# First loads on two queues, last outputs shared with GpSimd, last activations in another ring, one activation and one down product placed later

## The chip, the cores and the metric

The kernel runs on one core of one Trainium2 chip. The metric is the device time of one execution in microseconds (us). A core has TensorE (PE, matmuls; PEld is its weight load), VectorE (DVE), ScalarE (ACT), GpSimd (POOL) and SyncE (SP, which here only issues transfers). Each engine works through its own list of instructions in order and waits on semaphores for the others.

## The reference

A decoder trunk of two layers (`DEPTH`) on x of 512 tokens and 1024 features. Each layer mixes tokens with two kinds of attention, and then comes an MLP with a squared ReLU, the part that matters here; the last step is an RMSNorm.

```python
def hybrid_layer(x, norm_mix, w_in, ...):
    h = rmsnorm(x, norm_mix)
    proj = h @ w_in
    ...
    mixed = jax.nn.sigmoid(gate_a) * y_a + jax.nn.sigmoid(gate_b) * y_b
    x = x + mixed @ w_out
    h = rmsnorm(x, norm_mlp)
    return x + jnp.square(jax.nn.relu(h @ w_up)) @ w_down      # 1024 -> 4096 -> 1024

def reference(x, ..., norm_final):
    for l in range(DEPTH):
        x = hybrid_layer(x, ...)
    return rmsnorm(x, norm_final)
```

## The kernel before

Data lie transposed, features on the 128 partitions and the 512 tokens along the free axis, so x is eight tiles of 128x512. Every fp32 operand is split into a high part and the rest (`h`, `lo`), and a product is three matmuls per block of 128: high by high, high by low and low by high (L212 to L214 in `gemm`). ACT makes the high part by a cast (`wh` L186 for weights, `uh` L234 for x times gain, `sh` L1215 for the operands of the fast product, `oh` L1296 for activations); DVE makes the rest (`wl` L187, `ul` L235, `sl` L1216), but for the activations GpSimd does (`ol` L1297). PSUM has eight banks of 512 columns, which go by the tags mm, S, PT and O, two each, and are taken in turn by `bank()`.

Weights come by `fetch` (L170: a DMA of a plan's next piece into a buffer `raw`), then `convert` splits them into `wh` and `wl` one step ahead of their use.

**The MLP.** The first 8 of the 32 up products of a layer are made plainly. The other 24 are made in 12 units, g = 4 to 15, each of which gives two blocks of 128 features, called z and y, by seven half-size products (class `Strassen`, `unit`). One such product is eight matmuls (L1226). Products 0, 2 and 4 of a unit go to one bank `m`, one after the other, with ACT copying the bank out in between (L1250 for product 0, L1258 for product 2); products 1 and 6 share another (L1254). L1261 copies product 3. DVE puts the pieces together, `halves` (L1286) folds them, and `act` does Relu (L1294), Square (L1295) and the cast to `oh` (L1296) on ACT and the rest `ol` (L1297) on GpSimd. Meanwhile `convert` of the class makes the seven operands of the next unit, two of the sums on GpSimd (L1206, L1207).

The down products (`down`, twelve matmuls each: four blocks of activations by three; x takes them at L949) come in 48 pieces, six groups of eight; group c reads activations 4c to 4c+3. Twelve run ahead of the units. The others are placed between the products of the units: at each of four spots (ahead of products 2, 4 and 6 and at the end) `between` may run one, and a tuple says how many each unit gets. What is left runs after unit 15. The last eight activations (units 12 to 15) are read by a last set of products (`wdn`) after that.

The rings of buffers that matter: `oh` and `ol`, eight each (activations); `uh` and `ul`, eight each (x times gain, and the seven operands of a unit); `t2`, `raw`.

**The start.** `go` issues the transfer of the gains, then x and the halves of the first weight (`wva`) alternate on SP; 20 matmul instructions on a tile of ones (L1106) run while they come. `token_proj` (L315) makes the first products, x being the stationary side; per x tile it needs `uh`, `ul`, `wh` and `wl`.

**The tail.** The last layer's products are made in two halves of 256 tokens. `out(f)` works out the row factors R of half f by matmuls into a PSUM bank (`rstd`, L283), multiplies the eight tiles of x by R (L1067) and sends them out in five transfers (L1068).

An automatic scheduler in the toolchain puts the final order of each engine together from the program's order, so an instruction can stand elsewhere than the text has it.

Of the kernel before, what the change touches and what calls it, by code (L numbers as in the profile page):

```python
# [12 lines left out]
F32R = mybir.dt.float32r  # L13
AF = mybir.ActivationFunctionType
OP = mybir.AluOpType
AX = mybir.AxisListType

L = 2
D = 1024
T = 512  # L20
KT = D // 128
# [122 lines left out]
class Body:  # L144
# [19 lines left out]
    def fetch(self):  # L164

        if self.plan:
            src, n, *tag = self.plan.popleft()
            tag = tag[0] if tag else self.raws.popleft() if self.raws else "raw"
            raw = self.t(tag, [128, 1024], name="raw")
            self.nc.sync.dma_start(raw[:, :n], src)  # L170
            self.loaded.append((raw, src, n))

    def convert(self):
# [28 lines left out]

    spots = ()
    raws = deque()

    def gemm(self, ps, w, k0, xs, ks=8, start=True, stop=True):
        h, lo = w
# [85 lines left out]
    def token_proj(self, srcs, n, banks, u):  # L293
        mm = self.nc.tensor.matmul
        for c in range(4):
            first = len(srcs[c]) == 2
            parts = []
            for j in range(2):
                if len(u) <= 2 * c + j:
                    self.first_u(u, 2 * c + j)  # L300
                if first:
                    h, lo = self.weights(srcs[c][j], n)
                    parts.append((h[:, :n], lo[:, :n]))
            if not first:
                h, lo = self.weights(srcs[c][0], 2 * n)
                if len(srcs[0]) == 2 and c == 1:
                    self.setup()
                parts = [(h[:, j * n:(j + 1) * n], lo[:, j * n:(j + 1) * n]) for j in range(2)]
            for j in range(2):
                uh, ul = u[2 * c + j]  # L310
                h, lo = parts[j]
                first, last = c == 0 and j == 0, c == 3 and j == 1
                for b in range(NB):
                    s = slice(b * 128, (b + 1) * 128)
                    mm(banks[b][:, :n], uh[:, s], h, start=first, stop=False)  # L315
                    mm(banks[b][:, :n], uh[:, s], lo, start=False, stop=False)
                    mm(banks[b][:, :n], ul[:, s], h, start=False, stop=last)
                if j == 0:
                    self.ahead()
                yield  # L320
# [607 lines left out]
    def mlp(self, l, x, u, acc, gm):  # L928

        nc, a = self.nc, self.a  # L930
        R = None
        pend = []
        acts = []

        def act(ps):
            t = self.t("tmp", [128, T])
            nc.vector.scalar_tensor_tensor(t, ps, 0.0, R, op0=OP.max, op1=OP.mult)
            h = self.t("oh", [128, T], F32R)
            lo = self.t("ol", [128, T], F32R)
            nc.scalar.activation(t, t, AF.Square)  # L940
            nc.scalar.copy(h, t)
            nc.vector.tensor_tensor(lo, t, h.bitcast(F32), op=OP.subtract)
            acts.append((h, lo))

        def down(c, m, w):

            ps = self.bank()
            yield from self.gemm(ps, w, 4 * (m % 2), acts[4 * c:4 * c + 4], ks=4)
            nc.vector.tensor_add(x[m], x[m], ps)  # L949

        def downs():
            for c in range(6):
                for m in range(8):
                    if m % 2 == 0:
                        w = self.weights(a["wd2"][l, c, m // 2])
                    yield lambda: run(down(c, m, w))

        S = Strassen(self, l, x, gm)
        D = downs()
        raws = [None] * 16  # L960
        g0 = self.PLAIN // 2
        S.load(g0)
        for j in range(self.PLAIN):
# [12 lines left out]
            for _ in range(3):  # L976
                next(prep, None)
        conv = S.convert(g0)
        for i in range(12):
            next(D)()  # L980
            if i < 7:
                next(prep, None)
                next(prep, None)
            elif i == 7:
                run(prep)
            else:
                next(conv, None)
                next(conv, None)
            if i == 10:
                S.load(g0 + 1)  # L990
        run(conv)
        for g, n in zip(range(g0, 16), (2, 2, 3, 3, 4, 4, 4, 4, 4, 3, 1, 0)):
            S.load(g + 2)
            S.unit(g, D, n, acts)
        for d in D:
            d()
        u_next = []
        acts = acts[24:]
        if l + 1 < L:
            acc = []  # L1000
            self.load_small(l + 1)
            for m in range(8):
                ps = self.bank()
                w = self.weights(a["wdn"][l, m].rearrange("p k c -> p (k c)"))
                run(self.gemm(ps, w, 0, acts))
                nc.vector.tensor_add(x[m], x[m], ps)
                acc = self.sumsq(x[m], acc, m == 7)
                u_next.append(self.make_u(x[m], self.gain[:, 16 * l + 16:16 * l + 24], m))
                nc.scalar.dma_start(self.xs[m], x[m])
        else:  # L1010
            self.last(x, acts, a["wdn"][l])
        self.acc = acc
        return u_next

    def last(self, x, acts, wdn):


        nc, a = self.nc, self.a
        n = T // 2
# [39 lines left out]
            nc.scalar.activation(xm, xm, AF.Copy, scale=self.gain[:, 32 + m:33 + m])  # L1059

        def out(f, wait):
            R, _ = self.rstd(acc[f], (self.turn_tag(), self.turn_tag()), wait=wait, exp=False, copy=f == 0)
            for k, w in ((0, 1), (1, 1), (2, 2), (4, 2), (6, 2)):
                y = self.t("t2", [128, 2, n], name="y")[:, :w]
                for j in range(w):
                    eng = nc.gpsimd if f == 0 and k + j in (0, 3, 5, 7) else nc.vector
                    eng.tensor_tensor(y[:, j], x[k + j][:, f * n:(f + 1) * n], R, op=OP.mult)  # L1067
                nc.sync.dma_start(a["yT"][f, :, k:k + w], y)  # L1068

        acc = [[], []]  # L1070
        run(chain(*[products(0, m) for m in (0, 2, 3, 4, 5, 6, 7)]))
# [18 lines left out]
    def first_u(self, u, k):  # L1090
        x = self.t("t2", [128, T], name="x")
        self.nc.sync.dma_start(x, self.a["xT"][k])
        u.append(self.make_u(x, self.gain[:, :8], k))
        self.acc = self.sumsq(x, self.acc, k == KT - 1)

    def go(self):
        nc, a = self.nc, self.a
        self.gain = self.cp.tile([128, 40], F32, name="gain")
        nc.sync.dma_start(self.gain, a["gain"])
        self.ones2 = self.cp.tile([128, 2], F32, name="ones")  # L1100
        nc.vector.memset(self.ones2, 1.0)
        ones = self.t("tmp", [128, 128], name="ones")
# [9 lines left out]
        self.plan = deque(x for l in range(L) for x in self.order(l))  # L1112
        self.loaded, self.split = deque(), deque()
        self.raws = deque(("e", "e"))
        for l in range(L):
            u = self.layer(l, u)
            self.x_src = self.xs


class Strassen:  # L1120
# [9 lines left out]
    def __init__(self, body, l, x, gm):  # L1130
        self.b, self.nc, self.l, self.x, self.gm = body, body.nc, l, x, gm
        self.raw, self.ops = {}, {}

    def prepare(self, R):

# [94 lines left out]
    def unit(self, g, D, n, acts):  # L1230
        b, nc = self.b, self.nc
# [16 lines left out]
        m = product(0)  # L1248
        y = b.t("zz", [128, 2, 512], name="y")
        A.copy(y[:, 0], m)  # L1250
        next(conv, None)
        p5 = product(1)
        z = b.t("zz", [128, 2, 512], name="z")
# [9 lines left out]
        between()  # L1263
        product(4, m)
        V.tensor_tensor(z, z, m[:, None, :].to_broadcast([128, 2, 512]), op=OP.add)
        pair = [None, None]
        self.act(self.halves(z), pair, 0)
        next(conv, None)
        p2 = product(5)
        V.tensor_tensor(y[:, 0], p2, y[:, 0], op=OP.subtract)  # L1270
# [1 line left out]
        between()  # L1272
        product(6, p5)
        V.tensor_tensor(y[:, 1], y[:, 1], p5, op=OP.subtract)
        self.act(self.halves(y), pair, 1)
        acts += pair
        next(conv, None)
        between()
        for _ in conv:
# [6 lines left out]
        self.nc.vector.tensor_tensor(c.rearrange("p (k c) -> p k c", k=2), v[:, :, 0], v[:, :, 1], op=OP.add)  # L1286
        return c

    def act(self, c, pair, i):

        b, nc = self.b, self.nc
        h = b.t("oh", [128, T], F32R)
        lo = b.t("ol", [128, T], F32R)
        nc.scalar.activation(c, c, AF.Relu)  # L1294
        nc.scalar.activation(c, c, AF.Square)  # L1295
        nc.scalar.copy(h, c)  # L1296
        nc.gpsimd.tensor_tensor(lo, c, h.bitcast(F32), op=OP.subtract)  # L1297
        pair[i] = (h, lo)


def chain(*gens):
# [33 lines left out]
```

## Time and profile before

| | |
|---|---|
| time, median of 3 runs | 1535.23 us (1534.68 to 1535.87) |
| the profiled execution | 1534.54 us; span in the trace 1532.5 us |
| granted TensorE clock | 0.998 |
| PE busy | 1515.8 us, 99% of the span |
| DVE, ACT, POOL busy | 74%, 53%, 14% |

A timeline row gives start, length, engine, line, operation, output tile <- input tiles, shape, and in brackets the idle time ahead of it and what ended it. A row of waits gives who waited for what, the total in us, how often, and the longest. SPq is the queue of SP's instructions. PE matmuls are pipelined: the time from one start to the next counts, not the length.

```profile
span 1532.5 us, 21386 instructions
```

### The profile page before, as it was taken

To read this page: it belongs to the slowest core of one execution; us is meant where nothing else is said; L and a number is where in the kernel's file an instruction comes from. 1 tells how busy PE (TensorE), PEld (TensorE's weight loads), DVE (VectorE), ACT (ScalarE), POOL (GpSimd) and SP (SyncE) were. 2 spreads that over 40 slices of the span, in tenths; PEclk is the share of its full clock that TensorE was granted. 3 is DMA by queue.
4 is the path that set the end of the run, shared out by engine and by line. 5 is a ranking of instruction groups with operands and counts; after the bars stand their busy time and mean duration, and the time that the engine had idled before them with its cause. 6 is when DMAs were issued, how large, how long until landed. Compare 5 with 4: busy or idle time off the path is not lost.

```text
span 1532.5 us, 21386 instructions
## 1 busy us (share of the span) xinstructions
PE 1515.8 (99%) x7772; PEld 1270.9 (83%) x7772; DVE 1132.8 (74%) x2191; ACT 816.8 (53%) x1529; POOL 216.8 (14%) x178
## 2 busy tenths in 40 slices
PE   9999999999999999999999999999999999999997
PEld 8878888888888888888888788878888888888887
DVE  5588998866479887775646799887574989877753
ACT  6464665553454655555435556565434646555652
POOL 4000000000201332221300000000002023222222
PEclk9999999999999999999999999999999999999999
DMA  7655422143333333322546543222422333323221
GB/s 263 176 149 136 120 70 83 64 136 101 99 95 112 110 97 101 106 69 79 176 141 175 156 128 86 85 67 70 151 97 97 95 113 109 105 92 107 69 83 56
DMA packets 56633, 169.49 MB, mean 111 GB/s; under 512 B 7344, under 2 KB 8112, under 8 KB 56528
## 3 DMA queue, kind: packets, MB, share of 16 engines
q1 hardware_dynamic: 53072, 161.84, 34.5%
q10 hardware_dynamic: 3456, 6.29, 1.2%
q8 instruction: 61, 1.00, 0.3%
q14 instruction: 44, 0.36, 0.1%
HBM read 140.77 MB, written 4.19 MB: 95 GB/s over the span
## 4 chain that ended last, share of the span: by engine, by line
PE 90%; DVE 4%; ACT 3%; issue 1%; DMA 1%; POOL 1%; SPq 0%; DVEq 0%; ACTq 0%; POOLq 0%
PE ps_mm L212 12%; PE ps_mm L213 12%; PE ps_mm L214 12%; PE ps_S L1226 4%; PE ps_O L1226 4%; PE ps_O L447 4%; PE ps_PT L212 3%; PE ps_PT L214 3%; PE ps_PT L213 3%; PE ps_PT L421 3%; PE ps_PT L1226 3%; PE ps_mm L1226 3%; PE ps_S L213 2%; PE ps_S L214 2%; PE ps_S L212 2%; PE ps_O L213 2%
## 5 line engine op out<-in xcount | busy, mean ns | idle before, releaser
L186 ACT CAST wh<-raw 128x1024 fp32r<-128x1024 f32 (+2 forms) x187 | 192.4, 1029 | 251.7 <-PE ps_mm L213 66.0
L187 DVE TENSOR_TENSOR wl<-raw,wh 128x1024 fp32r<-128x1024 f32 (+2 forms) x187 | 225.3, 1205 | 55.1 <-ACT wh L186 54.0
L212 PE MATMUL ps_mm<-uh,wh 128*128 128x512 f32 x512 | 202.2, 395 | 0.0
L213 PE MATMUL ps_mm<-ul,wh 128*128 128x512 f32 x512 | 201.5, 394 | 0.0
L214 PE MATMUL ps_mm<-uh,wl 128*128 128x512 f32 x512 | 201.3, 393 | 0.0
L399 ACT ACTIVATE E<-E,mx 128x128 f32<-128x128 f32 x192 | 107.8, 562 | 65.8 <-DVE mx L398 62.7
L213 PE MATMUL ps_mm<-ol,wh 128*128 128x512 f32 (+1 forms) x316 | 122.9, 389 | 0.8 <-POOL ol L1297 0.8
L212 PE MATMUL ps_mm<-oh,wh 128*128 128x512 f32 (+1 forms) x316 | 122.9, 389 | 0.1
L214 PE MATMUL ps_mm<-oh,wl 128*128 128x512 f32 (+1 forms) x316 | 122.3, 387 | 0.0
L1216 DVE TENSOR_TENSOR sl<-s,sh 128x512 fp32r<-128x512 f32 x96 | 93.8, 980 | 34.3 <-ACT sh L1215 33.8
L430 ACT CAST pth<-ps_PT 128x512 fp32r<-128x512 f32 x144 | 72.9, 512 | 81.9 <-PE ps_PT L421 81.4
L214 PEld LDWEIGHTS ps_mm<-uh,wl 128*128 128x128 f32 x512 | 96.3, 188 | 19.9
L212 PEld LDWEIGHTS ps_mm<-uh,wh 128*128 128x128 f32 x512 | 96.2, 188 | 18.4 <-issue 1.5
L213 PEld LDWEIGHTS ps_mm<-ul,wh 128*128 128x128 f32 x512 | 96.6, 189 | 14.9
L398 DVE CUSTOM_DVE_ANT_0 E<-ps_S,ct 128x128 f32<-128x128 f32 x192 | 91.5, 481 | 21.6 <-PE ps_S L395 20.3
L431 DVE TENSOR_TENSOR ptl<-ps_PT,pth 128x512 fp32r<-128x512 f32 x144 | 85.5, 596 | 28.3 <-ACT pth L430 27.6
L253 POOL TENSOR_TENSOR acc<-sq 128x512 f32<-128x512 f32 (+1 forms) x6 | 8.1, 1356 | 578.6 <-DVE wl L187 565.7
L421 PE MATMUL ps_PT<-ct,E 128*128 128x128 f32 x480 | 83.5, 274 | 0.0
L1215 ACT CAST sh<-raw 128x512 fp32r<-128x512 f32 x72 | 44.7, 621 | 64.3 <-PE ps_PT L1226 24.7
L1215 ACT CAST sh<-s 128x512 fp32r<-128x512 f32 x96 | 59.5, 620 | 29.0 <-PE ps_S L1226 9.1
L1216 DVE TENSOR_TENSOR sl<-raw,sh 128x512 fp32r<-128x512 f32 x72 | 61.5, 854 | 14.7 <-ACT sh L1215 14.2
L421 PEld LDWEIGHTS ps_PT<-ct,E 128*128 128x128 f32 x480 | 60.1, 141 | 13.6 <-issue 3.7
(421 smaller groups left out, 3966.3 us busy)
## 6 DMA issues: line engine op xcount, KB each, us to landing
raw<-wb SPq DMA_DIRECT2D x64, 512.0 KB, 3.6
raw<-wup SPq DMA_DIRECT2D x64, 512.0 KB, 3.5
raw<-wd SPq DMA_DIRECT2D x48, 512.0 KB, 3.6
kd<-hl SPq DMA_DIRECT2D x48, 256.0 KB, 5.4
w<-w SPq DMA_DIRECT2D x32, 256.0 KB, 4.5
q<-hl SPq DMA_DIRECT2D x64, 128.0 KB, 2.6
raw<-wo SPq DMA_DIRECT2D x16, 512.0 KB, 3.6
raw<-wout SPq DMA_DIRECT2D x16, 512.0 KB, 3.5
```

Source lines behind the costliest of these rows:

```text
L186: nc.scalar.copy(h[:, :n], raw[:, :n])
L187: nc.vector.tensor_tensor(lo[:, :n], raw[:, :n], h[:, :n].bitcast(F32), op=OP.subtract)
L212: mm(ps, h[:, c], xh, start=start and i == 0, stop=False)
L213: mm(ps, h[:, c], xl, start=False, stop=False)
L214: mm(ps, lo[:, c], xh, start=False, stop=stop and i == ks - 1)
L398: nc.vector.tensor_tensor_reduce(e, ps[:, :n], self.mask[:, T - n:], -1.0, BIG, OP.add, OP.min, mx)
L399: nc.scalar.activation(e, e, AF.Exp, bias=mx, scale=-1.0, accum_out=sm[:, i:i + 1])
L421: nc.tensor.transpose(ps[:, j * 128:(j + 1) * 128], E[i][:, b * 128:(b + 1) * 128], self.ident)
L431: nc.vector.tensor_sub(lo[:, o:o + n], ps[:, :n], h[:, o:o + n].bitcast(F32))
L1215: nc.scalar.copy(h, src)
L1216: nc.vector.tensor_tensor(lo, src, h.bitcast(F32), op=OP.subtract)
L1226: mm = lambda o, w, x, **kw: self.nc.tensor.matmul(o, w, x, skip_group_check=True, **kw)
```

## The change

1. **Start.** The transfer of x tile 0 goes out first and the gains follow it. The first piece of weights (half 0 of `wva`) is issued by ACT instead of SP, ahead of ACT's table load. For the first chunk the square of x (`sumsq`) is placed behind the weight's conversion. In the scheduled order ACT then casts half 0 ahead of making `uh` of tile 0, and PE runs its products strictly bank by bank (high-high, high-low, low-high; before, four high-high products came first).
2. **Units.** The activation of y (Relu, Square, cast, `ol`) is kept and issued in the next unit behind the copy of product 0 (L1250); in unit 15 at once.
3. **Placement.** Unit 5 gets one down product instead of two, so each later down stands one place further back, and three instead of two run after unit 15.
4. **Ring.** In the last layer the activations of units 14 and 15 go into the `uh`/`ul` ring instead of the `oh`/`ol` ring.
5. **Tail.** R stays in PSUM for DVE; ACT makes a copy in SBUF for GpSimd in both halves. GpSimd makes tiles 6 and 7, sent from ACT's queue, DVE makes 0 to 5, sent from SP. (Before, in the first half GpSimd made 0, 3, 5 and 7 and R was copied to SBUF for all; in the second DVE made all eight from PSUM; SP sent everything.)

```diff
@@ fetch
-            self.nc.sync.dma_start(raw[:, :n], src)
+            eng = self.nc.scalar if self.first else self.nc.sync
+            self.first = False
+            eng.dma_start(raw[:, :n], src)
@@ token_proj
+                x = None
                 if len(u) <= 2 * c + j:
-                    self.first_u(u, 2 * c + j)
+                    x = self.first_u(u, 2 * c + j)
+                if x is not None and not first:
+                    self.acc = self.sumsq(x, self.acc, 2 * c + j == KT - 1)
                 if first:
                     h, lo = self.weights(srcs[c][j], n)
                     parts.append((h[:, :n], lo[:, :n]))
+                    self.acc = self.sumsq(x, self.acc)
@@ the units
-        for g, n in zip(range(g0, 16), (2, 2, 3, 3, 4, 4, 4, 4, 4, 3, 1, 0)):
+        for g, n in zip(range(g0, 16), (2, 1, 3, 3, 4, 4, 4, 4, 4, 3, 1, 0)):
@@ out
-            R, _ = self.rstd(acc[f], ..., wait=wait, exp=False, copy=f == 0)
-            for k, w in ((0, 1), (1, 1), (2, 2), (4, 2), (6, 2)):
+            R, _ = self.rstd(acc[f], ..., wait=wait, exp=False, copy=False)
+            r = self.t("r", [128, T], name="R")[:, :n]
+            nc.scalar.copy(r, R)
+            for k, w in ((6, 2), (0, 1), (1, 1), (2, 2), (4, 2)):
                 y = self.t("t2", [128, 2, n], name="y")[:, :w]
                 for j in range(w):
-                    eng = nc.gpsimd if f == 0 and k + j in (0, 3, 5, 7) else nc.vector
-                    eng.tensor_tensor(y[:, j], x[k + j][:, f * n:(f + 1) * n], R, op=OP.mult)
-                nc.sync.dma_start(a["yT"][f, :, k:k + w], y)
+                    eng, R_ = (nc.gpsimd, r) if k == 6 else (nc.vector, R)
+                    eng.tensor_tensor(y[:, j], x[k + j][:, f * n:(f + 1) * n], R_, op=OP.mult)
+                (nc.scalar if k == 6 else nc.sync).dma_start(a["yT"][f, :, k:k + w], y)
@@ first_u, go
         self.nc.sync.dma_start(x, self.a["xT"][k])
+        if k == 0:
+            self.nc.sync.dma_start(self.gain, self.a["gain"])
         u.append(self.make_u(x, self.gain[:, :8], k))
-        self.acc = self.sumsq(x, self.acc, k == KT - 1)
+        return x
...
-        nc.sync.dma_start(self.gain, a["gain"])
...
+        self.fetch()
         for l in range(L):
@@ unit
         A.copy(y[:, 0], m)
+        if self.rest is not None:
+            self.act(*self.rest)
         next(conv, None)
...
-        pair = [None, None]
-        self.act(self.halves(z), pair, 0)
+        tags = ("uh", "ul") if self.l == L - 1 and g > 13 else ("oh", "ol")
+        self.act(self.halves(z), acts, tags)
...
-        self.act(self.halves(y), pair, 1)
-        acts += pair
+        self.rest = self.halves(y), acts, tags
+        if g == 15:
+            self.act(*self.rest)
@@ act
-    def act(self, c, pair, i):
+    def act(self, c, acts, tags):
-        h = b.t("oh", [128, T], F32R)
-        lo = b.t("ol", [128, T], F32R)
+        h, lo = (b.t(tag, [128, T], F32R, name=n) for tag, n in zip(tags, ("oh", "ol")))
...
-        pair[i] = (h, lo)
+        acts.append((h, lo))
```

More of the change, by code (lines that the diff above doesn't have):

```diff
@@ L204 @@
     raws = deque()
+    first = True
     def gemm(self, ps, w, k0, xs, ks=8, start=True, stop=True):
@@ L1061, in out @@
         def out(f, wait):
-            R, _ = self.rstd(acc[f], (self.turn_tag(), self.turn_tag()), wait=wait, exp=False, copy=f == 0)
-            for k, w in ((0, 1), (1, 1), (2, 2), (4, 2), (6, 2)):
+            R, _ = self.rstd(acc[f], (self.turn_tag(), self.turn_tag()), wait=wait, exp=False, copy=False)
+            r = self.t("r", [128, T], name="R")[:, :n]
+            nc.scalar.copy(r, R)
+            for k, w in ((6, 2), (0, 1), (1, 1), (2, 2), (4, 2)):
                 y = self.t("t2", [128, 2, n], name="y")[:, :w]
                 for j in range(w):
-                    eng = nc.gpsimd if f == 0 and k + j in (0, 3, 5, 7) else nc.vector
-                    eng.tensor_tensor(y[:, j], x[k + j][:, f * n:(f + 1) * n], R, op=OP.mult)
-                nc.sync.dma_start(a["yT"][f, :, k:k + w], y)
+                    eng, R_ = (nc.gpsimd, r) if k == 6 else (nc.vector, R)
+                    eng.tensor_tensor(y[:, j], x[k + j][:, f * n:(f + 1) * n], R_, op=OP.mult)
+                (nc.scalar if k == 6 else nc.sync).dma_start(a["yT"][f, :, k:k + w], y)
         acc = [[], []]
@@ L1132, in __init__ @@
         self.raw, self.ops = {}, {}
+        self.rest = None
     def prepare(self, R):
```

## The prediction

> **What bounds the kernel now.** I read the page's busy shares first, then the table of busy time by stretches (length, then the busy time of PE, PEld, DVE, ACT and POOL), then the waits of PE (TensorE) in each stretch that had a gap.
>
> ```profile
> PE 1515.8 (99%) x7772; PEld 1270.9 (83%) x7772; DVE 1132.8 (74%) x2191; ACT 816.8 (53%) x1529; POOL 216.8 (14%) x178
> ```
> ```profile
> 498.00:735.00 237.00, 235.50 (x1179) 197.47 (x1178) 178.96 (x219) 134.11 (x222) 65.42 (x45) 1.00 0.30 96
> 1200.00:1480.00 280.00, 277.67 (x1382) 232.95 (x1381) 229.50 (x297) 160.11 (x263) 70.48 (x48) 1.00 0.32 102
> 1480.00:1533.00 53.00, 43.99 (x366) 43.65 (x364) 16.20 (x41) 17.66 (x39) 12.43 (x16) 0.95 0.13 49
> ```
>
> PE is the bound: 1515.8 us of the 1532.5 us span. The changed program issues the same matrix products (a few records more or less at the seams), so the change can only win time in which PE waits. That time lies in four stretches: before the first real matmul, in the MLP of layer 0 (498 to 735, 237.00 - 235.50 = 1.50 idle), in the MLP of layer 1 (280.00 - 277.67 = 2.33), and after the last matmul. The waits of PE in the two MLP stretches, and the readers of the copy at L1250 in the first, are:
>
> ```profile
> PE ps_S L1226 <- ACT y L1250: 0.6, 1, 0.6
> PE ps_S L213 <- POOL ol L1297: 0.5, 1, 0.5
> PE ps_O L1226 <- ACT y L1250: 0.2, 1, 0.2
> ...
>   PEld ps_mm L1226: 0.5, 1
> ...
> PE ps_mm L213 <- POOL ol L1297: 0.8, 2, 0.6
> PE ps_O L1226 <- ACT y L1250: 0.6, 1, 0.6
> PE ps_O L213 <- POOL ol L1297: 0.5, 1, 0.5
> PE ps_S L1226 <- ACT y L1250: 0.2, 1, 0.2
> ```
>
> So layer 0 has four stalls: three shown for PE, and one shown for the weight load alone (PEld ps_mm). Layer 1 repeats these four and has two more on `ol` at its end: six. Every one waits either for the copy at L1250 or for an `ol` that GpSimd (POOL) makes at L1297. The largest, in the order of time:
>
> ```profile
> 549.59 0.63 ACT L1294 ACTIVATE y<-y 128x512 f32<-128x512 f32 x1 [2.82 <-DVE y L1286]
> 550.25 0.40 PE L1226 MATMUL ps_PT<-t,sh 128*128 128x512 f32 x1
> 550.25 0.63 ACT L1295 ACTIVATE y<-y 128x512 f32<-128x512 f32 x1
> 550.48 0.28 PE L1226 MATMUL ps_PT<-t,sl 128*128 128x256 f32 x1
> 550.79 0.57 ACT L1250 COPY y<-ps_S 128x512 f32<-128x512 f32 x1
> 551.41 0.50 PE L1226 MATMUL ps_S<-t,sh 128*128 128x512 f32 x1 [0.65 <-ACT y L1250]
> 551.74 0.28 PE L1226 MATMUL ps_S<-t,sl 128*128 128x256 f32 x1
> ```
>
> ACT runs in order: it had to finish Relu and Square of the old unit's y (L1294, L1295) before it could copy product 0 of the new unit out of the bank that product 2 needs. The rows also give the true price. A 512-column matmul takes 0.23 of PE's time here (550.25 to 550.48) and a 256-column one 0.12, so without the wait the matmul of 551.41 would have started at 550.60: it is 0.81 late, and its own step of 0.33 (to 551.74) is 0.10 too long (0.23 is usual). Together 0.91, where the view reports 0.65. I take this 0.26 on top for every stall: layer 0 loses 1.50 + 4 x 0.26 = 2.54, layer 1 2.33 + 6 x 0.26 = 3.89.
>
> **The MLP, part by part.** The y activation now stands behind L1250 in ACT's order. At 551.41 this lets the copy start when product 0 ends (about 549.2, eight matmuls before 550.60), not at 550.79: with 0.57 it ends before product 1 does, and the stall goes whole. The two small L1250 stalls of each layer have the same cause (an `oh` or a weight cast of the old unit ahead of the copy) and go too.
>
> The price is that y's `oh`, and behind it `ol`, come later by about one product (4 x 0.35 = 1.40). In GpSimd's order `ol` of y moves behind the next unit's sum at L1206, 1.67 below. Who needs it early? Only the first down product that reads the acts of unit 5, and that is the other stall:
>
> ```profile
> 534.09 1.67 POOL L1206 TENSOR_TENSOR s<-raw 128x512 f32<-128x512 f32 x1 [0.63 <-DVE sl L1216]
> 535.73 1.73 POOL L1297 TENSOR_TENSOR ol<-y,oh 128x512 fp32r<-128x512 f32 x1
> 537.51 0.50 PE L213 MATMUL ps_S<-ol,wh 128*128 128x512 f32 x1 [0.49 <-POOL ol L1297]
> ```
>
> Here the down product placed later works: with one down fewer in unit 5, this down stands two products and a down later in PE's order, 2 x 1.40 + 12 x 0.23 = 5.5. The later `ol` costs at most 1.40 + 1.67 = 3.1 of it, so about 2.4 stays as cover and the stall goes. The ring buffer that z of units 8, 10 and 12 needs is now freed one place later, but still by the third matmul of a down that starts 1.40 after product 4, before z has passed DVE's add and ACT's Relu and Square. I take nothing for it.
>
> What is late next: the copy at L1250 of unit 6 has `sh` and `oh` of z ahead of it in ACT's new order, and now no down between products 0 and 2 to hide them. A 512-column step of ACT takes 0.57 to 0.63 in the rows above; product 1 (1.40) hides the copy (0.57) and one cast (0.63), not quite the copy and two. I take 0.2 per layer, between nothing and one cast with a restart, 0.63 + 0.26 = 0.9. Layer 0: 2.54 - 0.2 = 2.3.
>
> The end of layer 1:
>
> ```profile
> 1472.78 2.12 POOL L1297 TENSOR_TENSOR ol<-z,oh 128x512 fp32r<-128x512 f32 x1 [22.94 <-ACT oh L1296]
> ...
> 1477.34 2.27 POOL L1297 TENSOR_TENSOR ol<-y,oh 128x512 fp32r<-128x512 f32 x1
> 1477.43 0.38 PE L213 MATMUL ps_mm<-ol,wh 128*128 128x256 f32 x1 [0.60 <-POOL ol L1297]
> ```
>
> The last four acts had to wait for buffers that the last down frees, so GpSimd sat for 22.94 and then made four `ol` in a row, with PE close behind. In another ring they wait for no down; and three downs (3 x 12 x 0.23 = 8.3) instead of two stand between unit 15 and their use. The last one's way is two DVE steps (0.75 each, by the row of `ul` below, same shape), Relu, Square, `oh` and `ol`: about 1.5 + 3 x 0.63 + 2.27 = 5.7. Both stalls go. I take 0.1 off for unit 15, whose products are now interleaved otherwise and which has no downs left to hide a copy. Layer 1: 3.89 - 0.2 - 0.1 = 3.6. Layer 0 keeps the old ring at its end, where no stall shows: nothing.
>
> **The start.**
>
> ```profile
> 0.75 0.38 SPq L1099 DMA_DIRECT2D gain<-gain  x1
> 1.09 4.27 PE L1106 MATMUL ps_PT<-ones 128*128 128x128 f32 x20 [1.09 <-DVE ones L1103]
> 1.18 0.42 SPq L1092 DMA_DIRECT2D x<-xT  x1
> 1.65 0.90 SPq L170 DMA_DIRECT2D raw<-wva  x2
> 4.27 0.72 ACT L234 ACTIVATE uh<-x,gain 128x512 fp32r<-128x512 f32 x1 [2.04 <-DMA x<-xT]
> 5.03 0.75 DVE L235 SCALAR_TENSOR_TENSOR ul<-x,gain,uh 128x512 fp32r<-128x512 f32 x1 [3.46 <-ACT uh L234]
> 5.42 0.60 ACT L186 CAST wh<-raw 128x512 fp32r<-128x512 f32 x1
> 6.07 0.73 PE L315 MATMUL ps_S<-wh,uh 128*128 128x512 f32 x2 [0.71 <-ACT wh L186]
> ```
>
> x leaves SP 1.18 - 0.75 = 0.43 earlier, and the first weight half leaves ACT at about 0.75 instead of 1.65; both share the same transfer engines at once, so x lands 0 to 0.43 earlier. The square of x, which stood between `uh` (to 4.99) and the cast (from 5.42), leaves the path, and the cast of the half now stands ahead of `uh`. PE could start from 5.4 on, bounded by the warm-up matmuls that end at 1.09 + 4.27 = 5.36: at most 0.71 earlier. But the third matmul now needs `ul` (the old order ran four hi-hi products first): `uh` at 4.5 to 4.7 gives `ul` 0.76 later, to about 6.0 to 6.2, where the old third matmul stood at 6.07 + 0.45 = 6.52. I take 0.3, between -0.3 (the half lands after x and holds `uh` back on ACT) and 0.7. The memory traffic after it is the same, and the gain load is small. Table load and warm activation move back on ACT by one issue (about 0.4), inside the 2.04 that ACT waits ahead of `uh`.
>
> [...]
>
> **The tail.**
>
> ```profile
> L1067 POOL TENSOR_TENSOR y<-x,R 128x256 f32<-128x256 f32 x4 | 3.7, 932 | 8.2 <-ACT R L288 8.2
> 1526.29 2.74 DVE L1067 TENSOR_TENSOR y<-x,ps_O 128x256 f32<-128x256 f32 x8 [0.87 <-PE ps_O L283]
> 1526.74 2.65 SPq L1068 DMA_DIRECT2D yT<-y  x5
> ```
>
> Eight products on DVE become six: 2.74 x 6 / 8 = 2.06, so the last SP issue starts 0.68 earlier. Beside it ACT copies R (a 256-column copy; the 512-column copy took 0.57, so 0.3 to 0.6) and GpSimd makes two products at 0.93 (at best DVE's 0.42): 1526.29 + 0.3..0.6 + 0.8..1.9 = 1527.4 to 1528.8, against 1528.35 for DVE. The later of the two decides: gain 0.2 to 0.68; 0.93 is the row of the same instruction, which puts GpSimd at about 1528.6, so I take 0.5. The first half's outputs (out(0)) lie beside matmuls: its ACT issue holds ACT for two GpSimd products, 1.9 at most, while only squares of the second half are queued behind it. R kept in its bank of PSUM for 2.1 instead of one copy costs nothing, as a bank comes round after eight products.
>
> **Sum.** 0.3 + 2.3 + 3.6 + 0.5 = 6.7. The profiled execution took 1534.54 (span 1532.5, 2.0 around it): 1527.8. The median of the runs is 0.69 above it: 1528.5.
>
> **Rivals.**
>
> 1. The stalls come back elsewhere. For it: units 6, 7, 14 and 15 have few or no downs to hide a copy, and ACT's order still has casts near it. If three copies per layer are late by one cast with its restart, 0.9 each, 6 x 0.9 = 5.4 less the 0.5 already taken is given back: gain 1.8, 1533.4; with half of it 1531.0. Against: the copy now stands first after its product in most units.
>
> 2. The start gives hardly anything: x and the half share the way and land no earlier than x did, 4.27; then cast 0.60, `uh` 0.72 and `ul` 0.75 follow one another to 6.4, and the third matmul stands 0.1 earlier than 6.52. That is 0.2 less than taken, 1528.7; with -0.3 at the start, 1529.1. [...]
>
> 3. Slower: the weight cast in the full units. In the new order of ACT in units 8 to 12 the weight cast stands ahead of the copy of product 2 (before, it stood behind that of product 3), and product 4 waits for that copy.
>
> ```profile
> L186 ACT CAST wh<-raw 128x1024 fp32r<-128x1024 f32 x22 | 23.0, 1045 | 31.3 <-PE ps_mm L213 10.5 <-PE ps_O L1226 7.4 <-PE ps_PT L213 6.9
> ```
>
> The cast waits for the end of a down (L213), so ACT's queue would wait with it. Its cover is product 3 and a down, 1.40 + 2.73 = 4.1, and weight cast, one more cast and the copy take 1.05 + 0.63 + 0.57 = 2.3. If the buffer comes one down (2.73) later than I read, the copy is 2.3 + 2.7 - 4.1 = 0.9 late, 1.2 with restart, in ten units: 12 lost on top of the 6.7 won, 1528.5 + 12 = 1540.5. From 0.67 per unit nothing is won.
>
> **How the numbers follow.** 0.2% is 3.1 us, about what a measurement of this kernel can tell from no change. The forecast has 0.52 (1527.0 to 1529.8, from the bounds of its terms), rival 2 0.17 (near 1529), rival 1 0.24 (1530 to 1533.5, a third of it within 0.2%), rival 3 0.05; 0.02 is for no gain, where tail and start both lose. Faster by over 0.2% (below 1532.1) is 0.52 + 0.17 + 0.16 = 0.85; same 0.08 + 0.02 = 0.10; slower 0.05. The range of 8 in 10 leaves out 0.05 below 1526.8 (all terms at their best) and the upper part: 1532.3.
>
> **What would show it.** Right: no wait of PE on L1250 before 550 to 560, none on `ol` in either MLP, PE idle 0.5 or less in the two MLP stretches, first L315 matmul between 5.3 and 5.8 with a short wait for `ul` behind it, six DVE products in the last stretch and the span's end 3.1 us behind the last issue, as now (1532.5 - 1529.39). Wrong: waits of PE on L1250, L1254 or L1258 that recur in each unit (rival 3) or in units 6, 7, 14, 15 (rival 1).

## The result: slower by 0.14%, and the profile after

The changed kernel takes 1536.89 us (median of 22 runs, 1536.14 to 1539.03) where the kernel before takes 1535.03 (22 runs): a ratio of 1.0014, 95% interval 1.0007 to 1.0020. The forecast was 1528.5 with a range up to 1532.3. The profiled execution has a span of 1534.7 us (before: 1532.5), at the same granted clock, 0.998. The lines of the changed kernel moved: L1250 is now L1262, `act` L1294 to L1297 is L1308 to L1311, L1226 is L1238, and the tail's L1067 is L1076; `halves` L1286 is L1301, the cast `sh` L1215 is L1227, and the weight cast L186 is L188.

The table of busy time by stretches, of the changed kernel (length, then PE, PEld, DVE, ACT, POOL):

```profile
498.00:735.00 237.00, 233.92 (x1172) 196.26 (x1172) 177.05 (x220) 134.17 (x221) 68.58 (x45) 1.00 0.29 94
1200.00:1480.00 280.00, 276.94 (x1374) 232.47 (x1373) 227.10 (x298) 160.23 (x264) 73.78 (x48) 1.00 0.31 100
```

In the two MLP stretches PE idles 3.08 and 3.06 us, where it idled 1.50 and 2.33. Its waits there, first those of layer 0, then those of layer 1:

```profile
PE ps_S L1238 <- ACT y L1262: 1.7, 1, 1.7
PE ps_mm L1238 <- ACT y L1262: 1.3, 1, 1.3
...
PE ps_O L1238 <- ACT y L1262: 1.7, 1, 1.7
PE ps_PT L1238 <- ACT y L1262: 1.3, 1, 1.3
```

Every wait on `ol` is gone, as was forecast. But the copy of product 0, which was to be free, is now waited for 1.7 and 1.3 us in each layer. The first of these is in unit 6, the second in unit 7. ACT's own timeline around the two (layer 0), and the matmul that waits:

```profile
528.37 0.63 ACT L1308 ACTIVATE z<-z 128x512 f32<-128x512 f32 x1 [2.53 <-DVE z L1301]
528.91 0.60 ACT L1227 CAST sh<-raw 128x512 fp32r<-128x512 f32 x1
529.42 0.63 ACT L1309 ACTIVATE z<-z 128x512 f32<-128x512 f32 x1
529.95 0.60 ACT L1227 CAST sh<-s 128x512 fp32r<-128x512 f32 x1
530.46 0.61 ACT L1310 CAST oh<-z 128x512 fp32r<-128x512 f32 x1
530.98 0.57 ACT L1262 COPY y<-ps_S 128x512 f32<-128x512 f32 x1
531.61 0.49 PE L1238 MATMUL ps_S<-t,sh 128*128 128x512 f32 x1 [1.71 <-ACT y L1262]
...
548.26 0.63 ACT L1308 ACTIVATE y<-y 128x512 f32<-128x512 f32 x1 [2.19 <-DVE y L1301]
548.80 1.03 ACT L188 CAST wh<-raw 128x1024 fp32r<-128x1024 f32 x1
549.74 0.62 ACT L1309 ACTIVATE y<-y 128x512 f32<-128x512 f32 x1
550.26 0.56 ACT L1262 COPY y<-ps_mm 128x512 f32<-128x512 f32 x1
```

In unit 6 five instructions stand ahead of the copy, three of them the activation of **z** of unit 5, which the change didn't move. In the kernel before, ACT made Relu and Square of that z ahead of the same copy too, and the copy was in time:

```profile
528.92 0.40 PE L1226 MATMUL ps_PT<-b,sh 128*128 128x512 f32 x1
529.53 0.63 ACT L1294 ACTIVATE z<-z 128x512 f32<-128x512 f32 x1
530.72 0.57 ACT L1250 COPY y<-ps_PT 128x512 f32<-128x512 f32 x1
```

With a down less in unit 5, PE begins unit 6 at 526.56 instead of 528.92, 2.36 earlier, but Relu of z begins only 1.16 earlier (528.37 instead of 529.53): it waits for DVE's `halves`, and two casts `sh` and the `oh` of z now stand ahead of the copy. In unit 7 it is the Relu and Square of **y**, which the change was to move behind the copy, with a weight cast between them. The program's text has them behind; the scheduled order does not.

The starts of three matmuls (the first and the last one of a layer's units, and the very last one) divide the 2.2 us that the span has grown by. In each layer one down product, 12 x 0.23 = 2.73 us, now lies behind the units instead of among them; the table counts it with the units in both kernels:

| stage | before, us | changed, us | difference |
|---|---|---|---|
| start to the first unit product of layer 0 | 498.07 | 498.52 | +0.45 |
| units of layer 0 | 214.74 | 213.47 + 2.73 | +1.46 |
| to the first unit product of layer 1 | 540.77 | 543.39 - 2.73 | -0.11 |
| units of layer 1 | 214.75 | 213.52 + 2.73 | +1.50 |
| to the last matmul | 57.64 | 59.02 - 2.73 | -1.35 |
| to the end | 6.55 | 6.78 | +0.23 |

The tail of the changed kernel, in its timeline:

```profile
1528.24 0.37 ACT L1071 COPY R<-ps_O 128x256 f32<-128x256 f32 x1 [1.65 <-PE ps_O L286]
1528.69 1.41 POOL L1076 TENSOR_TENSOR y<-x,R 128x256 f32<-128x256 f32 x2 [5.47 <-ACT R L1071]
1528.70 2.08 DVE L1076 TENSOR_TENSOR y<-x,ps_O 128x256 f32<-128x256 f32 x6 [1.33 <-ACT R L1071]
1529.15 1.99 SPq L1077 DMA_DIRECT2D yT<-y  x4
1530.13 0.38 ACTq L1077 DMA_DIRECT2D yT<-y  x1
```

DVE's row says what went wrong: its first product is released by **ACT's copy** of R, not by PE, although it reads R from `ps_O` and not the copy. The copy runs from 1528.24 to 1528.61, and the products start 0.46 after it did. In the kernel before, where ACT makes no copy in this half, PE releases them.

And the start:

```profile
0.75 0.41 ACTq L172 DMA_DIRECT2D raw<-wva  x1
0.75 0.38 SPq L1101 DMA_DIRECT2D x<-xT  x1
4.93 0.62 ACT L188 CAST wh<-raw 128x512 fp32r<-128x512 f32 x1 [2.25 <-DMA raw<-wva]
5.46 0.72 ACT L237 ACTIVATE uh<-x,gain 128x512 fp32r<-128x512 f32 x1
6.23 0.58 PE L322 MATMUL ps_S<-wh,uh 128*128 128x512 f32 x1 [0.50 <-ACT uh L237]
7.02 0.50 PE L324 MATMUL ps_S<-wh,ul 128*128 128x512 f32 x1
```

The half on ACT's queue, issued 0.9 us earlier than before, is usable at 4.93; `uh` stands behind its cast and so starts 1.2 later than before (4.27). The first product comes at 6.23 instead of 6.07, and the third at 7.02.

### The profile page after: what moved, and what is told of

Same layout as the page of the kernel before. It is cut to its first block, busy times and chain, and to the rows that moved or that the text cites. A ratio compares the mean times of both kernels' runs of the same rounds, so it can differ in the third digit from the quotient of the medians.

```text
span 1534.7 us, 21405 instructions
## 1 busy us (share of the span) xinstructions
PE 1515.5 (99%) x7772; PEld 1271.0 (83%) x7772; DVE 1126.9 (73%) x2191; ACT 816.7 (53%) x1530; POOL 222.9 (15%) x178
## 5 line engine op out<-in xcount | busy, mean ns | idle before, releaser
L188 ACT CAST wh<-raw 128x1024 fp32r<-128x1024 f32 (+2 forms) x187 | 192.5, 1029 | 245.5 <-issue 65.2
L189 DVE TENSOR_TENSOR wl<-raw,wh 128x1024 fp32r<-128x1024 f32 (+2 forms) x187 | 234.0, 1251 | 58.9 <-ACT wh L188 58.2
L1228 DVE TENSOR_TENSOR sl<-s,sh 128x512 fp32r<-128x512 f32 x96 | 81.3, 850 | 41.2 <-ACT sh L1227 41.1
L216 PE MATMUL ps_mm<-ol,wh 128*128 128x512 f32 (+1 forms) x268 | 103.9, 388 | 0.0
L215 PE MATMUL ps_mm<-oh,wh 128*128 128x512 f32 (+1 forms) x268 | 103.7, 387 | 0.1
L217 PE MATMUL ps_mm<-oh,wl 128*128 128x512 f32 (+1 forms) x268 | 103.4, 386 | 0.0
L1227 ACT CAST sh<-raw 128x512 fp32r<-128x512 f32 x72 | 44.7, 621 | 59.6 <-PE ps_O L1238 19.2
L1227 ACT CAST sh<-s 128x512 fp32r<-128x512 f32 x96 | 59.5, 620 | 28.3 <-PE ps_PT L1238 8.0
L215 PE MATMUL ps_O<-oh,wh 128*128 128x512 f32 (+1 forms) x172 | 66.7, 388 | 0.0
```

The lines of the kernel that those rows point to most:

```text
L188: nc.scalar.copy(h[:, :n], raw[:, :n])
L189: nc.vector.tensor_tensor(lo[:, :n], raw[:, :n], h[:, :n].bitcast(F32), op=OP.subtract)
L215: mm(ps, h[:, c], xh, start=start and i == 0, stop=False)
L216: mm(ps, h[:, c], xl, start=False, stop=False)
L217: mm(ps, lo[:, c], xh, start=False, stop=stop and i == ks - 1)
L1227: nc.scalar.copy(h, src)
```

## The experiments

Two theories stood at the beginning: A, that the placement of the down products makes the new waits and the deferred activation of y hardly does anything; and B, that the deferred activation makes them. The expectations were written before the runs; medians of the kernel before were 1534.9 to 1535.1 beside them. The differences by stage are those of one profiled execution of each, by the same matmul starts as above; those of the start scatter between kernels that share a start (the first unit product of layer 0 came at 497.88 to 498.47 in nine kernels with the old start, mean 498.18, and at 498.19 to 498.54 in six with the new one, mean 498.44), so that stage is read with care.

**The placement alone.**

```diff
-        for g, n in zip(range(g0, 16), (2, 2, 3, 3, 4, 4, 4, 4, 4, 3, 1, 0)):
+        for g, n in zip(range(g0, 16), (2, 1, 3, 3, 4, 4, 4, 4, 4, 3, 1, 0)):
```

> The kernel before with one edit: unit 5 gets one down product instead of two (three run after unit 15). Theory A (the placement makes the new stalls): with a down less in unit 5, DVE and ACT fall behind and the copy of product 0 in units 6 and 7 comes late; PE waits some 1.9 and 1.5 us there in each layer, as in the changed kernel, and the time rises by about 2 x 1.5 = 3.0 us, less up to 1.4 at the end of layer 1 if the third down covers the two waits on ol there: 1536.6 to 1538. Theory B (the deferred activation of y makes them): no long wait on the copy here, the wait on ol in unit 6 gone, 1531 to 1533.

Measured: 1541.11 (1539.48 to 1543.41), ratio 1.0037, interval 1.0024 to 1.0049, which is over what either theory gave. Its waits of PE, layer 0 and then layer 1 with its end:

```profile
PE ps_S L1226 <- ACT y L1250: 1.6, 1, 1.6
PE ps_mm L1226 <- ACT y L1250: 1.3, 1, 1.3
PE ps_O L1226 <- ACT y L1250: 0.2, 1, 0.2
...
PE ps_mm L213 <- POOL ol L1297: 2.0, 2, 1.6
PE ps_O L1226 <- ACT y L1250: 1.6, 1, 1.6
PE ps_PT L1226 <- ACT y L1250: 1.3, 1, 1.3
PE ps_S L1226 <- ACT y L1250: 0.2, 1, 0.2
```

The two long waits are there without any deferral: B falls. The units lose 1.78 and 1.87 us. And the third down after unit 15 doesn't cover the last `ol`: while the buffers hang on the last down, a down more only moves the point at which they come free. Their wait even gets longer (2.0 us instead of 0.8). Counted from the start of the last down, the third of the four `ol`, for which PE waits longest, ends after 7.39 us instead of 6.18; it takes 2.25 instead of 1.27, and why stays open.

**The deferred activation alone.**

```diff
         A.copy(y[:, 0], m)
+        if self.rest is not None:
+            self.act(*self.rest)
...
-        self.act(self.halves(y), pair, 1)
+        self.rest = self.halves(y), acts
```

> The kernel before with one edit: the activation of y is issued in the next unit, behind the copy of product 0. Theory A: only the cast oh of y changes its place in ACT's scheduled order (Relu and Square stay ahead of the copy), so the waits of layer 0 stay as they are (0.8 and 0.3 us of delay in units 7 and 14, 0.4 in 15 may shrink): 1534 to 1535.2. Theory B: the waits on the copy grow to 1.9 and 1.5 us per layer: about 1538. The prediction's own reading (the copy stands first): 1531 to 1532.

Measured: 1534.39, ratio 0.9997 (0.9989 to 1.0006). By stage the units win 0.46 and 0.51 us: the small wait of unit 13 is gone, that of 14 is 0.2 instead of 0.4, and the wait of unit 7 and the one on `ol` in unit 6 are what they were. (The expectations call the two units of the small waits 14 and 15; counted by their products, 56 matmuls to a unit, they are 13 and 14.) In ACT's scheduled order only the cast `oh` of y changed its place, as theory A had it, and that from unit 8 on: in unit 7 it stood behind the copy before.

**The ring alone.**

```diff
+        tags = ("uh", "ul") if self.l == L - 1 and g > 13 else ("oh", "ol")
```

> The kernel before with one edit: the activations of units 14 and 15 of the last layer go into the uh/ul ring. Theory A: the two waits on ol at the end of layer 1 (0.37 and 0.77 us of delay with 0.1 of restart each) go by the ring alone: 1535.0 - 1.35 = 1533.7. Rival: they go by the third down that runs after unit 15, and the ring alone leaves them: 1535.0.

Measured: 1533.99, ratio 0.9991 (0.9982 to 1.0000). PE waits for no `ol` at the end of layer 1, and the stage after the last unit product is 0.94 shorter. In this execution the last four matmuls, those of R, took 1.20 us in their row instead of 0.68 (the last section has more on this), and the last one started 0.37 later for it than in the profile before; without that the ring wins 1.31. The rival, that it takes the third down, falls.

**The tail alone** (the new `out`, all else as before).

> The kernel before with one edit: the new tail. Theory A: DVE's first product waits for ACT's copy of R out of the same bank (0.45 us later), six products instead of eight win 0.66, and the last transfer takes 0.5 longer to land beside the one on ACT's queue: 0.2 us slower, 1535.2. The prediction's step: DVE starts as before and the time falls by 0.5, 1534.5.

Measured: 1534.83, ratio 0.9997 (0.9988 to 1.0006), which can't tell 0.2 us from nothing. The profile can: the stage from the last matmul to the end is 6.79 us; in all five profiled kernels with the new tail it is 6.78 to 6.93, in all eleven with the old one 6.50 to 6.67. (The upper values of both are those of executions in which the last four matmuls took about 1.2 us instead of 0.68: 6.92 and 6.93 against 6.66 and 6.67, where the others have 6.78 and 6.79 against 6.50 to 6.55.) In its timeline DVE waits for ACT again:

```profile
1527.01 2.08 DVE L1069 TENSOR_TENSOR y<-x,ps_O 128x256 f32<-128x256 f32 x6 [1.33 <-ACT R L1064]
```

**The start alone** (the edits of `fetch`, `token_proj`, `first_u` and `go`).

> The kernel before with one edit: the new start (x first, first weight half on ACT's queue, square of x behind the cast, products strictly bank by bank). Theory A: the half on ACT's queue lands no earlier for being issued 0.9 us earlier, since x and the other loads share the way, uh stands behind its cast, and the third product waits for ul: the first layer's products begin 0.16 and run on 0.45 to 0.6 later: 1535.5. The prediction's step: 0.3 earlier, 1534.7.

Measured: 1535.11, ratio 0.9999 (0.9991 to 1.0008); the first unit product at 498.35, within the scatter of the old start. It wins nothing that can be seen.

**The changed kernel with the old placement.**

> The changed kernel with the old placement (two downs in unit 5). Theory A: the long waits on the copy go (units 6 and 7: 1.98 and 1.58 us each layer with restart), the old ones of before come back (0.76 and 0.92), the end of layer 1 keeps its gain: 1536.9 - 2 x 1.5 = 1533.9. Theory B (deferred activation): the waits on the copy stay, 1536 to 1537.

Measured: 1533.33, ratio 0.9987 (0.9978 to 0.9996). One number turned back, from 1 to 2, brings 3.6 us.

**Deferred activation and ring alone** (old placement, start and tail).

> The changed kernel with the old start, the old placement and the old tail, that is the kernel before with the deferred activation and the ring alone. Theory A: the parts add up, so the start's 0.45 and the tail's 0.23 come back too: 1536.9 - 3.0 - 0.45 - 0.23 = 1533.2, faster than the kernel before by about 1.8 us.

Measured: 1533.09, ratio 0.9988 (0.9979 to 0.9997). Start and tail together make no difference to the run above that these runs can tell.

**Does the order on ACT make the waits?** What the change's text says was now enforced: an ordering edge, with no semaphore, from the copy to the activation of y.

```diff
-        A.copy(y[:, 0], m)
+        c0 = A.copy(y[:, 0], m)
         if self.rest is not None:
-            self.act(*self.rest)
+            with b.tc.issue_after(c0.ins):
+                self.act(*self.rest)
```

> The changed kernel, with the one addition that Relu, Square and cast of y may not be scheduled ahead of the next unit's copy of product 0. Theory A1 (it is the scheduler's order on ACT that makes the waits): the copy then stands first in units 7 to 15, the waits of unit 7 (1.58 us each layer with restart) and 14 and 15 (0.34 and 0.26) go; the wait of unit 6 (1.98) stays, since there the activation of z of unit 5 stands ahead. 1536.9 - 2 x 2.1 = 1532.7. Theory A2 (with one down less, DVE is behind and anything placed later only waits elsewhere): no change, 1536 to 1537.

Measured (all of the change, and this): 1532.75, ratio to the kernel before 0.9986 (0.9977 to 0.9995). PE's list of waits has none in units 7, 13 and 14; that of unit 6 stays, 1.85 and 1.87 late in the two layers. ACT's timeline in unit 7 now has the copy ahead of Relu of y (L1309 here):

```profile
548.16 0.62 ACT L1227 CAST sh<-s 128x512 fp32r<-128x512 f32 x1 [0.52 <-PE ps_mm L1238]
548.68 0.58 ACT L1262 COPY y<-ps_mm 128x512 f32<-128x512 f32 x1
549.16 0.63 ACT L1309 ACTIVATE y<-y 128x512 f32<-128x512 f32 x1
```

A1 holds, and by 4.1 us against the changed kernel.

The next run puts z of unit 5 behind that copy in the same way.

> As the run before it, and in unit 5 the activation of z is put behind the next unit's copy of product 0 too. Theory A1: the wait of unit 6 goes as well, 1536.9 - 2 x 4.0 = 1528.9; that would be the sum that the prediction made (1528.5) with the order that it took for given. Theory A2: the wait of unit 6 stays or turns into one on ol of unit 5: 1532 to 1533.

Measured: 1535.81 (1533.48 to 1538.32), ratio 1.0006 (0.9997 to 1.0015). The wait of unit 6 is gone, and unit 7 waits again, 2.6 us late in layer 0 and 2.4 in layer 1. Neither theory had that. The wait of PE in layer 0 and ACT's timeline ahead of it, with SP's issues:

```profile
PE ps_mm L1238 <- ACT y L1262: 2.4, 1, 2.4
...
542.75 7.50 SPq L172 DMA_DIRECT2D raw<-wd  x2
...
547.59 1.04 ACT L188 CAST wh<-raw 128x1024 fp32r<-128x1024 f32 x1 [4.04 <-DMA raw<-wd]
548.54 0.61 ACT L1227 CAST sh<-s 128x512 fp32r<-128x512 f32 x1
549.07 0.58 ACT L1262 COPY y<-ps_mm 128x512 f32<-128x512 f32 x1
```

A weight cast that stands ahead of the copy waits 4 us for its DMA, and the copy waits with it: the load was issued at 542.75, when DVE had done with the piece before it in that buffer (542.72), and was not there until 547.6. In the changed kernel the same load was issued at 541.20 and its cast came at 548.80, and no wait on a DMA showed. Here DVE comes to the piece before it later (from 541.51 instead of 539.97), so the load goes out 1.55 later, while ACT is ready for it at 543.55. With unit 6 faster the load has become the next thing that is late. The profiled execution is the fastest of the eleven, 2.3 us below the median; that this wait differs from run to run is likely, but not shown.

**The same with the old start and tail.**

> As the run before it, with the start and the tail of the kernel before. Theory A: the tail gives 0.23 back and the start 0.2 at most: 1528.5. The prediction's own steps for start and tail (0.3 and 0.5 won): 0.8 slower than the run before it.

Measured: 1534.59 (1533.16 to 1536.59), ratio 0.9999 (0.9990 to 1.0008). It is 1.2 us below the run before it, where theory A gave 0.4 below and the prediction's own steps 0.8 above. But the runs of both are spread over 3 to 5 us, and PE's wait in unit 7 differs between their two profiles, so what start and tail are worth can't be read from them. In this run's profile the weight cast waited 5.1 us, and PE was 3.7 late (below).

**Another placement.** Unit 5 keeps two downs; unit 6 gets two at its last spots instead of three (the 5 in the tuple stands for that), unit 7 four. With the enforced order for y, the ring, and the old start and tail.

```diff
-        places = iter({1: (1,), 2: (0, 1), 3: (1, 2, 3), 4: (0, 1, 2, 3)}.get(n, ()))
+        places = iter({1: (1,), 2: (0, 1), 3: (1, 2, 3), 4: (0, 1, 2, 3), 5: (2, 3)}.get(n, ()))
...
-        for g, n in zip(range(g0, 16), (2, 2, 3, 3, 4, 4, 4, 4, 4, 3, 1, 0)):
+        for g, n in zip(range(g0, 16), (2, 2, 5, 4, 4, 4, 4, 4, 4, 3, 1, 0)):
```

> The kernel before with the ring, with y's activation behind the next copy as in the runs beside it, and another placement: unit 5 keeps its two downs, unit 6 has two at its last two spots instead of three, unit 7 four instead of three. Theory A1: the down that waits for ol of unit 5 starts one product (1.4 us) later, the copy of unit 6 stands ahead of z's cast: no wait over 0.4 us in the units, 1533.1 - 2 x 1.7 = 1529.7. Theory A2: as the kernel with deferred activation and ring alone, 1533.

Measured: **1528.71** (1527.72 to 1529.41), ratio 0.9958 (0.9945 to 0.9970): 0.42% faster than the kernel before, and the lowest median of all. Its table of stretches:

```profile
498.00:735.00 237.00, 237.00 (x1191) 199.66 (x1190) 173.01 (x222) 136.25 (x224) 66.40 (x46) 1.00 0.30 97
1200.00:1480.00 280.00, 280.00 (x1426) 237.38 (x1425) 219.05 (x295) 161.41 (x266) 69.47 (x50) 1.00 0.33 101
```

PE has no idle time at all in either MLP. By stage the units win 2.61 and 2.61, the end of layer 1 1.32: 6.5 us, where the prediction's working had 2.54 + 3.89 = 6.4 to be won there.

**Order or placement?** The enforced order and the ring with the placement of before.

> The kernel before with the ring, and y's activation held behind the next unit's copy of product 0 (the placement of before). Theory A1: the copies of units 7, 14 and 15 stand first, their waits (0.9, 0 and 0.3 us each layer beside the kernel with deferred activation and ring alone) go; the wait on ol in unit 6 (0.76) stays: 1533.1 - 2 x 1.1 = 1530.9. So of the 4.4 us that the kernel with the other placement won over 1533.1, half would be the order on ACT and half the later down. Rival: the order alone wins nothing, 1533, and all came from the placement.

Measured: 1530.17, ratio 0.9967 (0.9954 to 0.9979). Only the wait on `ol` in unit 6 is left (0.65 late in each layer), and the units win 1.86 and 2.00. So of the 4.4 us between 1533.09 and 1528.71 the order brought about 2.9, the late down about 1.5.

**The new start on the best kernel**, and then with the first half on SP, ahead of x.

> The kernel with the other placement (two late downs in unit 6, y's activation held behind the copy, ring), now with the new start. Theory A: the first half on ACT's queue, although issued first, lands at about 4.9 us as in the changed kernel, uh follows it, and the time is the same or up to 0.3 us longer: 1528.7 to 1529.0. The prediction's step: 0.3 shorter, 1528.4.

> As the run before it, but the first half goes out on SP, ahead of x. Theory A (the two loads share the way, the queue does not matter): the half lands by about 4.9 or earlier, the first product comes within 0.3 us of the run before it. Rival (ACT's queue itself is late): the half lands about 0.9 earlier, like the 2.5 to 2.9 us that it took before, and the first product comes 0.5 or more earlier.

Measured: 1528.76, ratio 0.9959 (0.9946 to 0.9971), and 1529.35, 0.9961 (0.9948 to 0.9975): neither can be told from 1528.71. The start of the second, in its timeline:

```profile
3.51 0.62 ACT L186 CAST wh<-raw 128x512 fp32r<-128x512 f32 x1 [1.27 <-DMA raw<-wva]
4.40 0.63 ACT L244 ACTIVATE sq<-x 128x512 f32<-128x512 f32 x1 [0.27 <-DMA x<-xT]
5.69 0.50 PE L320 MATMUL ps_S<-wh,uh 128*128 128x512 f32 x1 [0.24 <-ACT uh L235]
6.98 0.62 ACT L186 CAST wh<-raw 128x512 fp32r<-128x512 f32 x1 [1.34 <-DMA raw<-wva]
```

Issued first on SP, the same half is usable at 3.51 instead of 4.94 in the first of the two, and x at 4.40. Both are there before the half alone is there by way of ACT's queue. The first product comes 0.54 earlier for it, as the rival had it, but then the second half is late (6.98) and the first unit product starts no earlier (498.8 against 498.5). Why the half on ACT's queue takes 4.2 us from its issue and not 2.7 is told by the packets (their number, MB, share of the 16 DMA engines) of the two queues in the first of the two runs, from 1.7 to 4.4 us:

```profile
q1 hardware_dynamic: 395, 0.50, 65.7%
q10 hardware_dynamic: 144, 0.26, 26.5%
```

q10 carries what ACT issues, here the half alone (0.26 MB); q1 carries what SP issues. So beside the half went x, the gains and most of the second half, 0.50 MB, and the two queues together took 92.2% of the 16 engines' time. In the second run, where the half is first in SP's one queue and x is issued behind it, at 1.20, the half was usable at 3.51. The half shares the way, as theory A had it, but with all that SP has queued, and not with x alone.

## Why the prediction was wrong, step by step

**What bounds the kernel** was right, with its prices: the ten waits were worth about 6.4 us, and the kernel that removes them all won 6.5 in those stages.

**The step that failed** is the first of the MLP part, "the y activation now stands behind L1250 in ACT's order". That is the order of the text. In the scheduled order Relu and Square of y, and mostly a weight cast, stayed ahead of the copy in units 7 to 14; only the `oh` cast stands behind it. The wait of unit 7, priced at 0.91 and taken as gone, became 1.58 with restart (with the deferral alone it stayed at 0.9, and the placement made it longer); the two small ones (units 13 and 14) shrank instead of going. The prediction speaks of ACT's new order for units 6 and 8 to 12, but not for its claim on unit 7.

**The second** is "what is late next" in unit 6: 0.2, at most 0.9, measured 1.98 (1.87 late and 0.11 of restart). The bound was one cast; ahead of the copy stood the whole activation of z and two casts. It was also misread where the missing down had stood: unit 6 had none between products 0 and 2 in the kernel before either (531.74 follows product 1 there without one). The down went from unit 5, ahead of its product 2, and it had given ACT and DVE the time for just that work: PE now comes to unit 6 2.36 earlier, Relu of z only 1.16. The gain from the later down, the `ol` wait of 0.76, was right and was paid for more than twice. These two terms, with what stayed of the small waits (about 0.6), turn -2.3 per layer into about +1.6; measured are +1.46 and +1.50.

**The end of layer 1** was right in sum (the stage is 1.35 shorter; the working had 0.8 of idle and 2 x 0.26, 1.3) but not in its cause: the ring alone wins 1.31 of it, the slower last four matmuls of its execution left out, and the third down alone made it worse.

**The tail** was forecast at -0.5 and came out at +0.23. The copy of R was costed as lying beside DVE's products; DVE waits for it, from 1528.24 to 1528.70, which takes back most of the 0.68; and the last transfer, with one on ACT's queue beside it, lands 2.96 after its issue instead of 2.46. In all five profiles with the new tail DVE's releaser is ACT's copy, with 0.46 between the two starts (1528.24 and 1528.70 here, 1526.55 and 1527.01 with the tail alone). Both read R out of `ps_O`; that this is why they follow one another is likely, but not shown.

**The start** was forecast as 0.3 won, between 0.3 lost and 0.7 won; by the means of the first unit product it is 0.26 lost, which the medians of the runs do not show. The lower bound was nearly right, and its mechanism was named: "the half lands after x and holds `uh` back on ACT". `uh` did stand behind the half's cast, 1.2 later than before.

**The rivals.** The first, that the stalls come back elsewhere, is what happened, priced too low: it counted one cast per late copy, where three (unit 7) and five (unit 6) instructions stood. The second, that the start gives hardly anything, came true, and the packets of the two queues bear out its reason, a shared way. The third, a weight cast ahead of a copy that waits, showed itself in unit 7 once unit 6 was mended, but ahead of the copy of product 0, for a DMA and not for a buffer, and in none of units 8 to 12.

## What to carry to other kernels

Where a scheduler puts the order together, moving a line of the program is a wish: read the scheduled order for every claim that something "now stands behind", and put an explicit ordering edge where it must hold. A piece of filler work taken out of one place to cover another also gives away what it covered at the first place; ask what the engines behind PE were doing in it. In this tail DVE's products on `ps_O` started 0.46 us after ACT's copy out of it, and released by it, in all five profiles: the copy that was costed "beside" them lay in series with them.

## What the runs showed of the hardware

One number was not expected. In the run with the old ends, PE waited 3.5 us in unit 7, and its clock fell behind that wait. The stretches around it, where the column before the last two is the granted clock:

```profile
540.00:547.00 7.00, 7.00 (x38) 5.91 (x36) 7.00 (x10) 2.41 (x4) 1.29 (x1) 1.00 0.45 148
551.50:555.20 3.70, 3.70 (x14) 3.16 (x13) 1.63 (x3) 2.77 (x6) 3.14 (x3) 0.54 0.46 142
555.20:560.00 4.80, 4.80 (x26) 4.01 (x25) 2.50 (x4) 1.65 (x3) 1.12 (x1) 1.00 0.36 109
```

The granted clock was 0.54 in the second of them and 1.00 in the two others. PE's rows show the same: from 551.81 to 555.21, 3.40 us, a 512-column and a 256-column matmul together took 0.64 (552.02 to 552.66), where they had taken 0.35 (551.21 to 551.56). Layer 0's units took 2.65 us more than in the run before: 1.07 for the longer wait (3.5 instead of 2.4 us) and about 1.5 for the slower matmuls (an estimate: 3.40 x (1 - 0.35 / 0.64) = 1.5).

In the run before it PE waited 2.4 us at the same place, and the clock was 1.00 in the same three stretches; it was 1.00 over 1200 to 1480 in the run with the old ends too, with a wait of 2.0 in it. Shorter waits were followed by slower matmuls all the same, at the end of the program. There the last four matmuls stand behind a wait of 1.36 or 1.37. They took 0.68 in seven profiles (the kernel before, the changed kernel, the placement, the tail and the start alone, and the two runs with z behind the copy), but 1.19 or 1.20 in four (the deferred activation alone, the ring alone, both together, and the changed kernel with the old placement); in the changed kernel with the enforced order for y the last three of them took 0.85. So the length of a wait alone does not tell whether the matmuls behind it are slower; what else decides it no run shows.
